# Making the sums of the down-projection's weights during the cross-attention instead of during its output projection

## The chip, the cores and the metric

The kernel runs on one core of one Trainium2 chip. A core has a matrix engine (TensorE, PE in the profile; PEld is its loading of stationary blocks), a vector engine (VectorE, DVE), an activation engine (ScalarE, ACT), GpSimd (POOL) and SyncE (SP), on whose queue all DMA transfers of this kernel are issued, in order. Each engine works through its own instructions in order and waits on semaphores. The metric is the device time of one launch in microseconds (us); the median of three runs of the kernel before is 2608.81 us (2608.45 to 2614.19).

## What is computed

Two layers on 1024 tokens of width 1024 in float32. Layer 0 mixes the tokens by attention, layer 1 by a pooling mixer; each layer then attends to 256 memory tokens and applies a gated MLP:

```python
def memory_cross_attention(h, mem_n, w_q, w_kv, w_o):
    q = (h @ w_q).reshape(b, s, X_HEADS, X_HEAD_DIM) * (X_HEAD_DIM ** -0.5)
    kv = mem_n @ w_kv
    ...
    p = jax.nn.softmax(scores, axis=-1).astype(v.dtype)
    o = jnp.einsum('bhsm,bmhd->bshd', p, v).reshape(b, s, D_MODEL)
    return o @ w_o

def conv_gated_ffn(h, w_up, conv_w, conv_b, w_down):
    u = h @ w_up
    up = jnp.pad(u, ((0, 0), (1, 1), (0, 0)))
    u = up[:, :-2] * conv_w[0] + up[:, 1:-1] * conv_w[1] + up[:, 2:] * conv_w[2] + conv_b
    gate, val = u[..., :D_FF], u[..., D_FF:]
    return (jax.nn.silu(gate) * val) @ w_down
```

`w_down` is 2816 x 1024. Each sub-layer is preceded by an RMS norm and followed by a residual add.

## The kernel before

**Products.** Every float32 product is made of three passes (`mm3`, L598): both factors are split into a high part (a copy by ACT, L513/L521) and a remainder (a subtraction by DVE, L516/L522/L525), and high x high, high x low and low x high are summed in PSUM. The up- and the down-projection of the MLP use, for 2 x 2 blocks, a scheme with seven products instead of eight. For the down-projection that scheme needs, of each of ten pairs q of 128-row blocks of `w_down` (NQ = 10), the four sums T1 to T4 of its 512-column halves: T1 = B12-B11, T2 = B22-T1, T3 = B22-B12, T4 = B21-T2. They are made once in each layer, ahead of their use, and parked in DRAM (`WT`, ten tensors of four 128x512 blocks).

**Staging.** All weights come through `scr`, a pool of six buffers of 128x1024 float32 (L506): one transfer of 512 KB on SP's queue, a high part by ACT, a remainder by DVE into one of the 20 slots R. A buffer is taken by the next `scr()` in turn, and the transfer into it waits until its last user is done. The residual rows X (eight tiles of 128x1024) stay in SBUF.

**Cross-attention** (`cross`, L990). The query projection goes over four column pieces c of `w_q` with two halves of the tokens and two blocks m each: a gemm (`cross_q`, L976) is 24 matmuls of 512 columns. After piece 0 the memory tokens are normed and turned (`memory_T`). Then eight pieces of `w_kv` (`memory_part`), the first four for the keys; each has two groups of 24 matmuls of 256 columns. Then scores, softmax, the other four pieces, and the values. In what order the instructions of this stage stand in the queues of their engines is decided at build time by a scheduler, from the order in which they are written and its own estimate of their times.

**Output projection of the cross-attention** (`ffn`, `ffn_main`, `begin`, L375). The order is written out by hand: sixteen steps, each a half row tile (n, t), n being the column half. A step's gemm is 24 matmuls into one PSUM bank; DVE adds it to X (L1102). When the second half of row tile t is done (n = 1), the finished row is written to DRAM (`rows`, L241: X to Xd, 512 KB), because the same tile is then normed in place (`norm`, L246) for the MLP; the norm thus waits for that write. ACT and POOL meanwhile make the row's mean square and its root (L582, L574, L576). In seven of the steps PE turns a normed tile by eight transposes (`turn`, L251), and DVE and ACT take the turned banks (`take1`, `take2`, L269, L274, L284). The body of a step:

```python
            gemm(n, t)
            free(n, t)
            u = turns.get(i)
            if u is not None:
                self.turn(u)
            extras.get(i, lambda: None)()
            add(n, t)
            if n:
                self.rows(t)
            ahead(i)
```

`ahead(i)` (L1234) is where the sums of `w_down` are made: at step i it takes two `scr` buffers and starts the two 512 KB loads of pair i (L1239); at step i it also makes the four sums of pair i-1 in place (L1244, DVE) and starts their four writes of 256 KB to `WT` (L1245). So steps 0 to 10 carry it. After `ahead` come `take1`, the norm and `take2` of the step on DVE's queue.

**The MLP** follows in an order that a planner (`Plan`) lays out from fixed costs. Its down-projection reads the sums back from `WT` (L1256), much later.

Of the kernel before, what the change touches and what calls it, by code (L numbers as in the profile page):

```python
# [10 lines left out]
F32 = mybir.dt.float32  # L11
F32R = mybir.dt.float32r
AF = mybir.ActivationFunctionType
OP = mybir.AluOpType
AX = mybir.AxisListType

P = 128
# [25 lines left out]
NQ = NF // 2 - 1  # L43
# [183 lines left out]
class Seven:  # L227
# [144 lines left out]
        return u.rearrange("p (t h c) -> p h t c", h=2, c=P)[:, h]  # L372


    def begin(self, gemm, add, free, between, ahead):  # L375


        late, split = self.late, self.split
        steps = ((0, 0), (0, 2), (1, 0), (1, 2), (0, 4), (1, 4), (0, 6), (1, 6),
                 (0, 1), (1, 1), (0, 3), (1, 3), (0, 5), (0, 7), (1, 5), (1, 7))  # L380
        turns = {3: 0, 4: 2, 6: 4, 8: 6, 10: 1, 12: 3, 15: 5}
        extras = {1: between, 11: lambda: self.first_load(0, 3), 12: lambda: self.first_load(1, 1),
                  13: lambda: [self.sum(0, n) for n in ("S1", "S2", "S3")],
                  14: lambda: (split(0, "A12", "A11"), late("T2", 1), late("T2", 3)),
                  15: lambda: late("T3", 1)}
        for i, (n, t) in enumerate(steps):
# [6 lines that stand above are left out]
            add(n, t)  # L393
            if n:
                self.rows(t)
            ahead(i)
            if u is not None:
                self.take1(u)
            if n:
                self.norm(t)  # L400
            if u is not None:
                self.take2(u)
# [76 lines left out]
class Kernel:  # L479
    def __init__(self, ctx, tc, a, out):  # L480
        self.ctx, self.tc, self.nc, self.a, self.out = ctx, tc, tc.nc, a, out
        pool = lambda name, **k: ctx.enter_context(tc.tile_pool(name=name, bufs=1, **k))
        self.cst = pool("cst")
        self.rp = pool("rslots")
        self.fp = pool("fp")
        self.st = pool("st")
        self.R = Slots([self.rp.tile([P, 2048], F32R, name=f"R{i}") for i in range(N_SLOTS)])
        nc = self.nc
        self.ident = self.cst.tile([P, P], F32, name="ident")
        make_identity(nc, self.ident)  # L490
        self.mh = self.cst.tile([P, 8], F32, name="mh")
        nc.vector.memset(self.mh, -0.5)

# [495 lines left out]

    def cross(self, i, hT, qT, ws):  # L990
        nc, R = self.nc, self.R
        for c in range(XH):
            if c == 1:
                mT = self.memory_T(i)
            if c:
                ws = self.cross_piece(i, c)
            for half in range(2):
                if (c, half) not in qT:
                    self.cross_q(qT, c, half, ws, hT)
                if c == XH - 1:  # L1000
                    R.put(*hT[half])
            R.put(*ws)
        kT, v, memory_part = self.memory(i, mT)
        for c in range(4):
            memory_part(c)
        kh, kl = (R.v(s, 8) for s in kT)
        vh, vl = (R.v(s, 2) for s in v)
        prs, PT, O = {}, {}, []

        def scores(t):  # L1010
            half = t // 4
            tc_ = slice((t % 4) * P, (t % 4 + 1) * P)
            s = self.psA().rearrange("p (h m) -> p h m", h=XH)
            for h in range(XH):
                qv = R.tiles[qT[h, half]].rearrange("p (m i n) -> p m i n", m=2, i=2)
                for k in range(2):
                    self.mm3(s[:, h], qv[:, k, 0, tc_], qv[:, k, 1, tc_], kh[:, 2 * h + k], kl[:, 2 * h + k],
                             k == 0, k == 1)
            nm = self.stat(4, "nm4")
            nc.vector.tensor_reduce(nm, s, axis=AX.X, op=OP.max, negate=True)  # L1020
            pr = prs[t] = self.scr()
            p3 = pr.rearrange("p (h m) -> p h m", h=XH)
            rs = self.stat(4, "sum4")
            for h in range(XH):
                nc.scalar.activation(p3[:, h], s[:, h], AF.Exp, bias=nm[:, h:h + 1], accum_out=rs[:, h:h + 1])
            ri = self.stat(4, "inv4")
            nc.vector.reciprocal(ri, rs)
            for h in range(XH):
                nc.gpsimd.tensor_scalar(p3[:, h], p3[:, h], ri[:, h:h + 1], 1.0, op0=OP.mult, op1=OP.mult)
            if t % 4 == 3:  # L1030
                R.put(*(qT[h, half] for h in range(XH)))

        def turn(t):
            if t < 2:
                PT[t] = [R.get() for _ in range(4)]
            self.transposed(prs.pop(t), self.put_T(PT[t % 2], t // 2))

        def values(half, ms):
            pt = PT[half]
            if not ms[0]:  # L1040
                O.append([R.get() for _ in range(4)])
            o = O[half]
            for m in ms:
                p = self.psB()
                cols = slice(m * P, (m + 1) * P)
                for k in range(2):
                    bh, bl = self.blk(pt, (m // 2) * 2 + k, slice(0, 512))
                    self.mm3(p, vh[:, k, cols], vl[:, k, cols], bh, bl, k == 0, k == 1)
                h, l = self.blk(o, m, slice(0, 512))
                self.hi_lo(h, l, p)  # L1050
            if ms[-1] == NK - 1:
                R.put(*pt)

        for t in range(4):
            scores(2 * t)
            memory_part(4 + t)
        for t in range(4):
            scores(2 * t + 1)
            turn(2 * t)
        values(0, (0, 1))  # L1060
        turn(1)
        values(0, (2, 3))
        turn(3)
        turn(5)
        values(0, (4, 5))
        turn(7)
        values(0, (6, 7))
        values(1, range(NK))
        R.put(*kT, *v)
        return O  # L1070


    def conv_table(self, i):
        nc, a = self.nc, self.a
        cw = self.scr()
        c3 = cw[:2 * NF, :512].rearrange("p (j c) -> p j c", j=4)
        nc.sync.dma_start(out=c3[:, :3], in_=a["ffn_conv_w"][i].rearrange("j (f c) -> f j c", c=P))
        nc.sync.dma_start(out=c3[:, 3], in_=a["ffn_conv_b"][i].rearrange("(f c) -> f c", c=P))

        def turn():  # L1080
            cp = self.psB()[:, :4 * 2 * NF].rearrange("p (j f) -> p j f", j=4)
            for j in range(4):
                nc.tensor.transpose(cp[:, j, :], c3[:, j, :], self.ident[:2 * NF, :2 * NF])
            self.cv = self.cst.tile([P, 4, 2 * NF], F32, name="conv")
            nc.vector.tensor_copy(self.cv, cp)
        return turn
# [27 lines left out]
    def ffn_main(self, i, U, X, Xd, late, begin):  # L1114
        nc, R = self.nc, self.R
        wd = self.a["ffn_w_down"][i]
        G = self.tc.dram_tile([2 * P, S], F32, name=f"G{i}")
        G7 = self.tc.dram_tile([NQ, P, 7 * 512], F32, name=f"Gs{i}")
        WT = [self.tc.dram_tile([4, P, 512], F32, name=f"Wt{i}_{q}") for q in range(NQ)]
        C, fixed, half = {}, {}, U.half  # L1120


# [107 lines left out]


        WD, raws = {}, {}

        def ahead(i):  # L1234

            if i < NQ:
                raws[i] = [self.scr() for _ in range(2)]
                for j in range(2):
                    nc.sync.dma_start(out=raws[i][j], in_=wd[(2 * i + j) * P:(2 * i + j + 1) * P, :])  # L1239
            if 0 < i <= NQ:  # L1240
                (b11, b12), (b21, b22) = ((r[:, :512], r[:, 512:]) for r in raws.pop(i - 1))
                for n, (out, p, q) in {"T1": (b11, b12, b11), "T3": (b12, b22, b12), "T2": (b22, b22, b11),
                                       "T4": (b21, b21, b22)}.items():
                    nc.vector.tensor_tensor(out=out, in0=p, in1=q, op=OP.subtract)  # L1244
                    nc.sync.dma_start(out=WT[i - 1][int(n[1]) - 1], in_=out)  # L1245

        WAT = (("B21", "B22"), ("B11",), ("T1", "T2"), ("T3", "T4"))

        def plan_W(plan, q, late):
            def fetch(j):  # L1250
# [4 lines left out]
                else:  # L1255
                    nc.sync.dma_start(out=raws[q, j].rearrange("p (n c) -> p n c", n=2),  # L1256
                                      in_=WT[q][2 * (j - 2):2 * (j - 1)].rearrange("n p c -> p n c"))

# [80 lines left out]
            plan.add("add", 1024, low, [o, *parts], parts, uses=[o], late=late)  # L1339

        def main():
            begin(ahead)
            U.H["T4"] = [R.get(), R.get()]
            plan = Plan({"DVE": 6.5, "ACT": 4.9}, {"scr": 2, "A": 2, "B": 4, "half": len(R.freed)})
            for f, js in ((0, (0, 1, 2)), (1, (0,))):
# [19 lines left out]
            for item in order:  # L1365
# [7 lines left out]
                n, f = item  # L1373
# [17 lines left out]
        with self.tc.manual_schedule():  # L1391
            main()
# [211 lines left out]
```

## Time and profile before

| | |
|---|---|
| median of three runs | 2608.81 us (2608.45 to 2614.19) |
| the profiled execution | 2610.45 us, of which the span of its instructions is 2608.7 us |
| mean granted clock of PE | 0.989 |
| output projection of the cross-attention, layer 0 | about 847 to 956 us of the span |
| the same, layer 1 | about 1853 to 1960 us |
| query projection and keys of the cross-attention, layer 0 | about 659 to 769 us |
| the same, layer 1 | about 1669 to 1774 us |

Times inside the execution are us from the start of the span. In a row of the timeline the columns are the start, the length, the engine, the line of the kernel, the operation with its output and inputs, the count, and in brackets how long the engine had been idle and what ended that. A row of the chain of waits has start, length and what it was. "SPq" is the issue of a transfer by SP, which is short; the transfer itself is "DMA" in the chain. In the table by stretches each engine has its busy time in the stretch, with the number of its instructions.

### The profile page before, as it was taken

Reading aid. Unit: us, or ns where it says so; the run is one execution under the profiler, and the core shown is the slowest. Engines: PE = TensorE matmul, PEld = TensorE weight load, DVE = VectorE, ACT = ScalarE, POOL = GpSimd, SP = SyncE. Lnnn points to the kernel's source line nnn. Section 1 sums busy time; section 2 is a strip of 40 time slices with the busy share of each in tenths; the row PEclk is TensorE's granted clock in tenths of the full one; section 3 lists DMA queues with packets and bytes.
Section 4 is the critical chain, followed back from the end, with each engine's and each line's share of the span. In section 5 each row is a group of like instructions: output and inputs, shape, how many; then the busy total and the mean of one; then the engine's idle time right before and its main releaser. Section 6 shows DMA issues by size and latency. Waiting matters only on the chain.

```text
span 2608.7 us, 36701 instructions
## 1 busy us (share of the span) xinstructions
PE 2536.9 (97%) x13577; PEld 2166.9 (83%) x13577; DVE 1911.3 (73%) x2791; ACT 1298.5 (50%) x2192; POOL 378.1 (14%) x521
## 2 busy tenths in 40 slices
PE   7999999999999999999999998999999999999998
PEld 7988888888898778888887887889778888887886
DVE  5778999974336679888888765534769988888775
ACT  4448888852236246554555424524426555555441
POOL 3664555530002000000000001102010000000001
PEclk9999999999999999999999999999999999999999
DMA  4200000031313733433348642311673343337751
GB/s 155 82 9 1 1 2 1 2 138 40 98 56 117 279 124 113 122 101 99 104 158 268 208 153 76 120 62 44 226 243 100 92 120 101 106 100 264 236 189 65
DMA packets 279945, 298.41 MB, mean 114 GB/s; under 512 B 11605, under 2 KB 225981, under 8 KB 279765
## 3 DMA queue, kind: packets, MB, share of 16 engines
q1 hardware_dynamic: 279765, 296.06, 35.3%
q8 instruction: 107, 1.75, 0.3%
q14 instruction: 73, 0.60, 0.1%
HBM read 218.85 MB, written 72.35 MB: 112 GB/s over the span
## 4 chain that ended last, share of the span: by engine, by line
PE 76%; DVE 11%; DMA 4%; ACT 4%; issue 3%; POOL 2%; SPq 0%; DVEq 0%; ACTq 0%; POOLq 0%
PE pB L603 20%; PE pB L602 20%; PE pB L601 20%; PE pB L595 3%; PE pA L603 3%; PE pA L601 3%; PE pA L602 3%; DVE nm L681 2%; PE pA L677 2%; DMA scr<-in_ffn_w_down 1%; DMA Xd<-X 1%; PE pB L908 1%; DVE PT L522 1%; POOL qn L753 1%; PE pB L909 1%
## 5 line engine op out<-in xcount | busy, mean ns | idle before, releaser
L601 PE MATMUL pB<-R,R 128*128 128x512 f32 (+1 forms) x2728 | 1023.1, 376 | 4.5 <-ACT R L521 1.9
L603 PE MATMUL pB<-R,R 128*128 128x512 f32 (+1 forms) x2748 | 1025.0, 373 | 1.7 <-DVE R L516 1.7
L602 PE MATMUL pB<-R,R 128*128 128x512 f32 (+1 forms) x2728 | 1018.0, 373 | 1.7 <-DVE R L522 1.4
L601 PEld LDWEIGHTS pB<-R,R 128*128 128x128 f32 x2728 | 515.9, 189 | 98.6 <-ACT R L521 3.1
L603 PEld LDWEIGHTS pB<-R,R 128*128 128x128 f32 x2748 | 519.5, 189 | 93.7 <-DVE R L516 2.5
L602 PEld LDWEIGHTS pB<-R,R 128*128 128x128 f32 x2728 | 516.2, 189 | 92.6 <-DVE R L522 4.0
L513 ACT ACTIVATE R<-scr 128x512 fp32r<-128x512 f32 (+2 forms) x250 | 176.0, 737 | 211.2 <-PE pB L602 68.8
L574 POOL TENSOR_SCALAR ms<-ss 128x1 f32<-128x1 f32 (+2 forms) x102 | 26.7, 262 | 1671.9 <-ACT scr L582 758.8
L516 DVE TENSOR_TENSOR R<-X,R 128x512 fp32r<-128x512 f32 x310 | 209.7, 685 | 65.7 <-ACT R L513 65.6
L513 ACT ACTIVATE R<-X 128x512 fp32r<-128x512 f32 x310 | 193.3, 630 | 82.9 <-PE pB L602 62.2
L516 DVE TENSOR_TENSOR R<-scr,R 128x512 fp32r<-128x512 f32 (+2 forms) x250 | 197.9, 821 | 19.4 <-ACT R L513 19.4
L595 PE MATMUL pB<-ident,scr 128*128 128x128 f32 x1376 | 182.3, 276 | 9.6 <-DVE scr L587 8.0
L595 PEld LDWEIGHTS pB<-ident,scr 128*128 128x128 f32 x1376 | 157.0, 142 | 36.6 <-POOL scr L687 14.8
L687 POOL TENSOR_SCALAR scr<-scr,inv 128x1024 f32<-128x1024 f32 x128 | 144.2, 1127 | 167.1 <-DVE inv L686 162.2
L522 DVE TENSOR_TENSOR PT<-pB,PT 128x512 fp32r<-128x512 f32 x256 | 163.8, 680 | 3.4 <-ACT PT L521 2.4
L365 ACT COPY scr<-pB 128x512 f32<-128x512 f32 x132 | 77.4, 586 | 177.5 <-PE pB L603 175.2
L684 ACT ACTIVATE scr<-pA,nm 128x1024 f32<-128x1024 f32 x128 | 142.9, 1117 | 44.6 <-DVE nm L681 42.5
L1296 DVE TENSOR_TENSOR X<-pB,X 128x512 f32<-128x512 f32 x144 | 99.2, 690 | 87.8 <-PE pB L603 85.3
L601 PE MATMUL pA<-R,R 128*128 128x512 f32 (+1 forms) x448 | 156.3, 349 | 6.0 <-ACT R L521 2.1
L521 ACT ACTIVATE R<-pB 128x512 fp32r<-128x512 f32 (+1 forms) x182 | 94.5, 551 | 129.9 <-PE pB L603 82.1
L681 DVE TENSOR_REDUCE nm<-pA 128x1 f32<-128x1024 f32 x128 | 156.1, 1219 | 0.9 <-PE pA L677 0.5
L603 PE MATMUL pA<-R,R 128*128 128x512 f32 (+1 forms) x448 | 155.3, 347 | 1.1 <-DVE R L522 0.8
(138 smaller groups left out, 3647.9 us busy)
## 6 DMA issues: line engine op xcount, KB each, us to landing
X<-in_ffn_w_up SPq DMA_DIRECT2D x82, 512.0 KB
scr<-in_ffn_w_down SPq DMA_DIRECT2D x64, 512.0 KB
Gs<-X SPq DMA_DIRECT2D x100, 256.0 KB
scr<-Gs SPq DMA_DIRECT2D x56, 384.0 KB
Wt<-scr SPq DMA_DIRECT2D x80, 256.0 KB
scr<-Wt SPq DMA_DIRECT2D x40, 512.0 KB
scr<-in_xattn_w_kv SPq DMA_DIRECT2D x32, 512.0 KB
scr<-Gs SPq DMA_DIRECT2D x28, 512.0 KB
```

The source lines that it names most:

```text
L513: self.nc.scalar.activation(hi, src, AF.Copy)
L516: self.nc.vector.tensor_tensor(out=lo, in0=src, in1=hi.bitcast(F32), op=OP.subtract)
L521: nc.scalar.activation(hi, src, AF.Copy)
L522: nc.vector.tensor_tensor(out=lo, in0=src, in1=hi.bitcast(F32), op=OP.subtract)
L595: self.nc.tensor.transpose(p[:, k, :], src[:, b * P:(b + 1) * P], self.ident)
L601: mm(out, ah, bh, start=start, stop=False)
L602: mm(out, ah, bl, start=False, stop=False)
L603: mm(out, al, bh, start=False, stop=stop)
L681: nc.vector.tensor_reduce(nm, s, axis=AX.X, op=OP.max, negate=True)
L684: nc.scalar.activation(pr, s, AF.Exp, bias=nm, accum_out=rs)
L687: nc.gpsimd.tensor_scalar(pr, pr, ri, 1.0, op0=OP.mult, op1=OP.mult)
L1296: nc.vector.tensor_tensor(out=x, in0=banks[b], in1=x, op=OP.add)
```

## The change

The function `ahead` leaves `ffn_main` and becomes `down_sums`, which `cross` calls at its start. It returns a function that does on each call what a step did before: the loads of the next pair, and the sums and writes of the pair before. It is called after each `cross_q` that `cross` issues (seven: the first half of piece 0 is issued ahead of `cross`) and after each of the first four `memory_part` (four), eleven calls in each layer. The sums themselves and their number are as before; `ffn_main` gets the list through `self.WT`.

```diff
-    def begin(self, gemm, add, free, between, ahead):
+    def begin(self, gemm, add, free, between):
...
             add(n, t)
             if n:
                 self.rows(t)
-            ahead(i)
             if u is not None:
                 self.take1(u)
...
+        self.WT = {}
...
     def cross(self, i, hT, qT, ws):
         nc, R = self.nc, self.R
+        ahead = self.down_sums(i)
         for c in range(XH):
             if c == 1:
                 mT = self.memory_T(i)
...
                 if (c, half) not in qT:
                     self.cross_q(qT, c, half, ws, hT)
+                    ahead()
...
         for c in range(4):
             memory_part(c)
+            ahead()
...
+    def down_sums(self, i):
+        nc, wd = self.nc, self.a["ffn_w_down"][i]
+        WT = self.WT[i] = [self.tc.dram_tile([4, P, 512], F32, name=f"Wt{i}_{q}") for q in range(NQ)]
+        raws, todo = {}, iter(range(NQ + 1))
+
+        def ahead():
+            q = next(todo, None)
+            if q is None:
+                return
+            if q < NQ:
+                raws[q] = [self.scr() for _ in range(2)]
+                for j in range(2):
+                    nc.sync.dma_start(out=raws[q][j], in_=wd[(2 * q + j) * P:(2 * q + j + 1) * P, :])
+            if q:
+                (b11, b12), (b21, b22) = ((r[:, :512], r[:, 512:]) for r in raws.pop(q - 1))
+                for n, out, x, y in ((0, b11, b12, b11), (2, b12, b22, b12), (1, b22, b22, b11), (3, b21, b21, b22)):
+                    nc.vector.tensor_tensor(out=out, in0=x, in1=y, op=OP.subtract)
+                    nc.sync.dma_start(out=WT[q - 1][n], in_=out)
+        return ahead
...
-        WT = [self.tc.dram_tile([4, P, 512], F32, name=f"Wt{i}_{q}") for q in range(NQ)]
+        WT = self.WT.pop(i)
...
-            begin(ahead)
+            begin()
```

More of the change, by code (lines that the diff above doesn't have):

```diff
@@ L1232, in ffn_main @@
         WD, raws = {}, {}
[L1234 to L1245, printed above, removed]
         WAT = (("B21", "B22"), ("B11",), ("T1", "T2"), ("T3", "T4"))
```

## The prediction

> **What bounds the kernel now.** The page first:
>
> ```profile
> span 2608.7 us, 36701 instructions
> PE 2536.9 (97%) x13577; PEld 2166.9 (83%) x13577; DVE 1911.3 (73%) x2791; ACT 1298.5 (50%) x2192; POOL 378.1 (14%) x521
> PE 76%; DVE 11%; DMA 4%; ACT 4%; issue 3%; POOL 2%; SPq 0%; DVEq 0%; ACTq 0%; POOLq 0%
> ```
>
> PE is busy for 97% of the span and holds 76% of the chain of waits. The change leaves PE's instructions and their order alone (the built programs show the same list), so it can only act where PE waits or runs slowly. The table by stretches says where that is: first the output projections of both layers, then the query projection and the key pieces, layer 0 and layer 1.
>
> ```profile
> core 0: us, PE busy (x) PEld busy (x) DVE busy (x) ACT busy (x) POOL busy (x), PEclk, DMA share, GB/s
> 853.50:956.40 102.90, 94.55 (x419) 77.05 (x417) 63.73 (x90) 22.74 (x41) 9.29 (x16) 0.93 0.68 235
> 1858.90:1959.80 100.90, 93.35 (x418) 76.11 (x418) 63.66 (x90) 22.83 (x41) 8.74 (x16) 0.95 0.70 241
> 659.00:745.00 86.00, 85.50 (x388) 70.28 (x386) 24.65 (x31) 23.34 (x34) 0.74 (x2) 1.00 0.20 64
> 745.00:769.00 24.00, 23.99 (x200) 23.98 (x200) 10.68 (x15) 6.92 (x13) 0.00 (x0) 1.00 0.42 132
> 1669.00:1750.00 81.00, 80.50 (x366) 66.16 (x364) 24.06 (x31) 23.19 (x35) 0.74 (x2) 1.00 0.21 70
> 1750.00:1774.00 24.00, 24.00 (x200) 24.00 (x201) 10.58 (x15) 7.37 (x13) 0.00 (x0) 1.00 0.42 131
> ```
>
> In the output projections PE idles 8.35 and 7.55 us, its granted clock is 0.93 and 0.95, and the DMA engines are busy 0.68 and 0.70 of the time. In the cross-attention PE hardly idles (0.5 us), its clock is 1.00, DMA stands at 0.20 and 0.42, and DVE at 24.65 of 86 us. So work leaves a crowded stage for an empty one.
>
> What PE waits for is shown by its waits in the two output projections (total, times, longest) and by one piece of the chain:
>
> ```profile
> PE pB L251 <- DVE X L246: 8.4, 3, 3.8
> PE pB L251 <- DVE X L246: 7.5, 4, 3.1
> ...
> 869.79 0.70 DVE X L1102
> 870.51 6.36 DMA Xd<-X
> 877.00 1.30 DVE X L246
> ...
> 878.34 1.26 PE L251 MATMUL pB<-ident,X 128*128 128x128 f32 x8 [2.23 <-DVE X L246]
> 880.34 0.63 PE L603 MATMUL pB<-R,R 128*128 128x512 f32 x1
> 880.77 0.63 PE L601 MATMUL pB<-R,R 128*128 128x512 f32 x1
> 884.21 0.39 PE L602 MATMUL pB<-R,R 128*128 128x512 f32 x1
> 884.44 0.40 PE L603 MATMUL pB<-R,R 128*128 128x512 f32 x1
> ```
>
> A row is finished (L1102), its write to Xd takes 6.36 us, only then may it be normed in place, and PE's transposes wait 2.23 us for that. After such a wait matmuls start every 0.43 us instead of every 0.23 us for some 4 us: each wait is paid about twice.
>
> **The loss in numbers.** L1102 marks the end of each gemm, as long as DVE is free for it:
>
> ```profile
> 852.87 0.69 DVE L1102 TENSOR_TENSOR X<-pB,X 128x512 f32<-128x512 f32 x1 [2.63 <-PE pB L603]
> 858.94 0.68 DVE L1102 TENSOR_TENSOR X<-pB,X 128x512 f32<-128x512 f32 x1
> 864.35 0.69 DVE L1102 TENSOR_TENSOR X<-pB,X 128x512 f32<-128x512 f32 x1 [1.95 <-PE pB L603]
> 869.79 0.69 DVE L1102 TENSOR_TENSOR X<-pB,X 128x512 f32<-128x512 f32 x1 [0.36 <-PE pB L603]
> 892.38 0.69 DVE L1102 TENSOR_TENSOR X<-pB,X 128x512 f32<-128x512 f32 x1 [0.37 <-PE pB L603]
> 898.70 0.69 DVE L1102 TENSOR_TENSOR X<-pB,X 128x512 f32<-128x512 f32 x1 [0.66 <-PE pB L603]
> 955.75 0.69 DVE L1102 TENSOR_TENSOR X<-pB,X 128x512 f32<-128x512 f32 x1
> 1858.26 0.69 DVE L1102 TENSOR_TENSOR X<-pB,X 128x512 f32<-128x512 f32 x1 [2.24 <-PE pB L603]
> 1959.10 0.69 DVE L1102 TENSOR_TENSOR X<-pB,X 128x512 f32<-128x512 f32 x1
> ```
>
> A step without a turn takes 869.79-864.35 = 5.44 us; one with a turn 898.70-892.38 = 6.32, so a turn is 0.88; the first gap, with the turn of the convolution's table in it, is 6.07, or 0.63 more. From the first add to the last lie 15 gemms, six turns and that table: 15x5.44 + 6x0.88 + 0.63 = 87.5 us. The trace has 955.75-852.87 = 102.9 and 1959.10-1858.26 = 100.8. Lost: 15.4 + 13.3 = 28.7 us. (Cross-check for layer 0: 8.35 idle and 0.07x102.9 = 7.2 of clock make 15.6.)
>
> **What is removed.** In both layers together:
>
> ```profile
> L1244 DVE TENSOR_TENSOR scr<-scr x80: 678/692/721, 859.5 to 1927.9; 128x512 f32<-128x512 f32 x80
> L1239 SPq DMA_DIRECT2D scr<-in_ffn_w_down x40: 327/424/1325, 842.1 to 1920.2; - x40
> L1245 SPq DMA_DIRECT2D Wt<-scr x80: 319/422/1329, 860.2 to 1928.6; - x80
> ...
> 916.27 6.42 DMA scr<-in_ffn_w_down
> 950.31 0.69 DVE L1102 TENSOR_TENSOR X<-pB,X 128x512 f32<-128x512 f32 x1 [2.35 <-PE pB L603]
> 953.77 1.28 DVE L246 SCALAR_TENSOR_TENSOR X<-X,rs,scr 128x1024 f32<-128x1024 f32 x1 [2.77 <-DMA Xd<-X]
> ```
>
> Per layer: 40 subtractions (40x0.69 = 27.7 us of DVE), 20 loads and 40 writes, 21 MB. Two effects go with them. The write of a row no longer shares the DMA engines with 2 MB in each step: late in the stage, with that traffic over, the norm starts 953.77-950.31-0.69 = 2.77 us after the add instead of 7. And DVE no longer stands before a load: at 916.27 the chain runs through a load of 6.42 us, behind which the takes of the turned banks and the next add were queued.
>
> Does a wait stay? From the end of a gemm: add 0.69, write 2.77, norm 1.28, with some 0.1 of gaps 4.85 us. Between that gemm and the turn that needs the row, PE has at least one other gemm, 5.44 us. So no wait should be left, with 0.6 us to spare. What is late next is the row's root on ACT and POOL: in the quiet row the write, not the root, came last, so the root takes less than 2.77. The three subtractions of an odd turn (3x0.69) and its two remainders fit into the 5.44 us as well. The spare is thin, and two loads of the up-projection now start near the write of row 1, so I leave 0.5 us a layer: 28.7 - 1.0 = 27.7 us gained, between 28.7 (no wait, no slow clock) and 8.4 + 7.5 = 15.9 (the idle alone goes).
>
> **What is added.** The same 120 transfers and 80 subtractions, in the cross-attention. DVE has room: 24.65 + 10.68 + 27.7 = 63 of 110 us. DMA too: 21 MB more over 110 us is 190 GB/s on top of 64 and 132. The danger is order. In the built program DVE's subtractions stand between the drains of the query gemms; each waits for its load, and the drain behind it waits along.
>
> ```profile
> 707.01 0.69 DVE L525 SCALAR_TENSOR_TENSOR R<-pB,R 128x512 fp32r<-128x512 f32 x1 [3.38 <-ACT R L524]
> 712.46 0.69 DVE L525 SCALAR_TENSOR_TENSOR R<-pB,R 128x512 fp32r<-128x512 f32 x1 [4.75 <-ACT R L524]
> 742.61 3.49 DVE L522 TENSOR_TENSOR R<-scr,R 128x1024 fp32r<-128x1024 f32 x3 [2.26 <-ACT R L521]
> 756.66 0.42 DVE L522 TENSOR_TENSOR R<-pB,R 128x256 fp32r<-128x256 f32 x1 [2.46 <-ACT R L521]
> 759.54 0.42 DVE L522 TENSOR_TENSOR R<-pB,R 128x256 fp32r<-128x256 f32 x1 [2.46 <-ACT R L521]
> ```
>
> A drain comes every 5.44 us with 4.75 us of idle before it; four subtractions fit in 2.8. There are four banks, so a drain may be three gemms (16 us) late before PE stops. SP's queue and `scr`: the eleven calls take 20 of the buffers that the weights use, and a weight load now stands behind the writes of a pair. The tightest such load is the fourth key piece: its buffer comes free with the three remainders at 742.61+3.49 = 746.1; with 6.42 us of landing and 2.3 for high and low part it is there at 755. Groups of that stage are 759.54-756.66 = 2.88 us apart, and the fourth piece begins at about 762. Even at the worst landing nothing is late by these rows, so the cost is 0 at best; for what I can't see (queueing of loads behind writes) I take 0.5 us a layer, and 7.3 us a layer as its upper end: the landing excess of 6.42-2.77 = 3.65, twice.
>
> On that queueing the Trainium skill speaks against the change: in "DMA: Bandwidth & Descriptors", section "Queues, rings and completion order", it says that each DMA engine consumes a queue's descriptors in ring order. A weight load issued behind four writes would then land after them as well. The trace agrees: 6.36 us behind 2 MB, 2.77 us alone; the sum stays, since the worst landing is in it.
>
> **Sum.** 2610.45 (the profiled execution, 1.74 more than its span, and 1.64 over the median) - 28.7 + 1.0 + 1.0 = 2583.8; against the median, 2608.8 - 26.7 = 2582.1 us. I predict 2582.
>
> **Rivals.** (1) Slower: the `scr` loop paces PE. A call needs load, sums and writes before its buffers serve again: 2.77 + 2.8 + 6.36 = 11.9 us if calls don't overlap, and eleven have the 110 us of query projection and keys, 10 each. Then 22x(11.9-10) = 42 is lost against 27 won: 2624. It decides from 11.6 us a call, where 22x1.6 = 35 eats the gain and 8 more. For it: one SP queue, six buffers. Against: the built order issues a second pair's loads ahead of the first pair's last writes, so two calls overlap. 7%. (2) The key pieces become DMA-bound: 1 MB of weights, 1 MB loaded and 1 MB written in 5.76 us is more than the 241 GB/s moved at a share of 0.70, or 344 at full share: 3.15 MB take 9.1 us, 3.4 too many, in four pieces and two layers 27 us: 2609, no change. Against: the pieces' loads start earlier, where PE needs 22 us for each query piece. 5%. (3) The slow clock is not the waits' doing and stays: only 8.4 + 7.5 of idle go, 2593. For it: 2.23 us is a short wait to slow a clock. Against: it is 1.00 in every stretch above without waits. 6%.
>
> The skill's page "TensorE: Matmul & The Clock Gate", section "Part 1: The HAM clock gate (the "warmup" mystery)", says that the clock halves after an idle window of about 3.4 us. By that rule a 2.23 us wait need not slow it, which is the third rival; the trace, slow right behind that wait, disagrees.
>
> (4) The write stays slow without the traffic, and only the waits for loads in DVE's queue go (the longest waits, 3.8 and 3.1, each paid twice: 13.8): 2595. Against: the 2.77. 4%.
>
> **How the numbers follow.** Forecast 78% (2578 to 2590). The range 2577 to 2600 takes in rivals 3 and 4 and the upper end of the added cost (2582 + 2x6.8 = 2596); below it ends 5 us under the forecast, since no more than 28.7 is there to be had and runs differ by a few us. A measurement of this kernel can tell about 0.3%, 8 us, from no change. Faster than 2601: 78+6+4 = 88%; within: rival 2, 5%; slower: 7%.
>
> **What would show it.** In the output projections: adds 5.44 and 6.32 us apart throughout, 88 to 89 us from first to last, clock 1.00, DMA share about 0.2, the norm 2.8 to 3.1 us after its add. In the cross-attention: the subtractions of `down_sums` between the drains, DMA share 0.6 or more, PE's idle still under 1 us and adds and drains 5.44 apart. Waits of PE for remainders of weights there, or for drains, would prove me wrong; so would norms that still start 5 us after their add.

## The result, and the profile after

| | before | after |
|---|---|---|
| median of the runs, us | 2609.29 (2608.45 to 2614.19, 4 runs) | 2585.19 (2584.72 to 2586.67, 4 runs) |
| after to before | | 0.9905, 95% interval 0.9888 to 0.9922 |
| span of the profiled execution, us | 2608.7 | 2583.3 |
| first to last add of the output projection, layer 0 / layer 1, us | 102.9 / 100.8 | 88.2 / 88.15 |

The changed kernel is 0.95% faster, 24.1 us by the medians and 25.4 by the spans. Line numbers shift with the moved code: the add of the output projection is L1126 now (L1102 before), the subtractions L1093 (L1244), their writes L1094 (L1245), the loads L1089 (L1239), the drain of a query gemm L524 (L525), the add of the down-projection L1306 (L1296).

The first lines of its page, span and busy time (share of the span, number of instructions):

```profile
span 2583.3 us, 36696 instructions
...
PE 2524.0 (98%) x13577; PEld 2156.9 (83%) x13577; DVE 1910.4 (74%) x2791; ACT 1298.5 (50%) x2192; POOL 379.5 (15%) x521
```

DVE and ACT are busy for as long as before: nothing was saved, only moved. PE shows 13 us less busy time for the same 13577 matmuls. Of these, 11.7 us are in the two output projections (94.55 and 93.35 before, 88.08 and 88.09 in the next table), whose granted clock was 0.93 and 0.95: the same work ran more slowly there.

The table by stretches of the changed kernel, for the same four stages as in the prediction (both output projections, the query projection and the key pieces of layer 0):

```profile
core 0: us, PE busy (x) PEld busy (x) DVE busy (x) ACT busy (x) POOL busy (x), PEclk, DMA share, GB/s
852.30:940.60 88.30, 88.08 (x419) 72.79 (x418) 37.26 (x50) 22.44 (x41) 7.79 (x16) 1.00 0.18 60
1845.00:1933.20 88.20, 88.09 (x419) 72.75 (x418) 37.33 (x50) 22.44 (x41) 7.78 (x16) 1.00 0.18 60
658.00:744.00 86.00, 85.49 (x388) 70.29 (x387) 48.02 (x66) 24.58 (x36) 2.45 (x4) 1.00 0.81 283
744.00:768.00 24.00, 24.00 (x201) 24.00 (x202) 12.89 (x19) 6.62 (x13) 0.00 (x0) 1.00 0.66 217
```

In the output projections PE idles 0.2 and 0.1 us where it idled 8.35 and 7.55, its clock is 1.00, and the DMA share fell from 0.7 to 0.18. In the cross-attention DMA's share rose from 0.20 to 0.81 and from 0.42 to 0.66, and DVE's busy time doubled in the first stretch, while PE's column stands to the hundredth: 85.49 of 86.00 (85.50 before), 24.00 of 24.00.

Adds and norms of the changed kernel's first output projection, by their start; in brackets the idle time of DVE before the instruction and what ended it:

```profile
851.67 0.69 DVE L1126 TENSOR_TENSOR X<-pB,X 128x512 f32<-128x512 f32 x1 [2.63 <-PE pB L602]
...
866.66 1.29 DVE L246 SCALAR_TENSOR_TENSOR X<-X,rs,scr 128x1024 f32<-128x1024 f32 x1 [2.81 <-DMA Xd<-X]
...
904.86 0.69 DVE L1126 TENSOR_TENSOR X<-pB,X 128x512 f32<-128x512 f32 x1 [3.01 <-PE pB L602]
909.14 1.28 DVE L246 SCALAR_TENSOR_TENSOR X<-X,rs,scr 128x1024 f32<-128x1024 f32 x1 [3.59 <-DMA Xd<-X]
910.34 0.68 DVE L1126 TENSOR_TENSOR X<-pB,X 128x512 f32<-128x512 f32 x1
917.11 0.69 DVE L1126 TENSOR_TENSOR X<-pB,X 128x512 f32<-128x512 f32 x1 [1.30 <-PE pB L602]
...
939.89 0.69 DVE L1126 TENSOR_TENSOR X<-pB,X 128x512 f32<-128x512 f32 x1
```

The norm now starts 2.8 to 3.6 us after its add (909.14 is 3.59 behind the end of the add at 904.86), where the second row of the kernel before took 6.5 (877.00 against 869.79+0.69). The last add is at 939.89, 88.2 us behind the first. The step 917.11-910.34 = 6.77 is the one that is still too long beside the 6.34 or so of the other steps with a turn (one add that DVE makes late, 7.03 us and then 4.87, aside), a residue of some 0.4 us behind the latest norm, 3.59. Right behind that row's write, SP issues two loads of the up-projection (905.99 and 906.47).

And DVE in the query projection of the changed kernel, where the subtractions went:

```profile
722.14 0.69 DVE L524 SCALAR_TENSOR_TENSOR R<-pB,R 128x512 fp32r<-128x512 f32 x1 [4.15 <-ACT R L523]
...
727.58 0.69 DVE L1093 TENSOR_TENSOR scr<-scr 128x512 f32<-128x512 f32 x1 [4.75 <-DMA scr<-in_ffn_w_down]
728.19 0.68 DVE L524 SCALAR_TENSOR_TENSOR R<-pB,R 128x512 fp32r<-128x512 f32 x1
```

DVE stands before loads here too, 4.75 us at 727.58 with the drain of 728.19 queued behind. That drain is 0.6 us later than 5.44 behind its predecessor, and PE does not notice: the query gemms change between banks of PSUM. Here the wait of DVE costs nothing; how far that cover reaches is tested below.

### The profile page after: what moved, and what is told of

It is laid out like the page before. It is cut to its first block, busy times and chain, and to the rows that moved or that the text cites. A ratio compares the mean times of both kernels' runs of the same rounds, so it can differ in the third digit from the quotient of the medians.

```text
span 2583.3 us, 36696 instructions
## 1 busy us (share of the span) xinstructions
PE 2524.0 (98%) x13577; PEld 2156.9 (83%) x13577; DVE 1910.4 (74%) x2791; ACT 1298.5 (50%) x2192; POOL 379.5 (15%) x521
## 5 line engine op out<-in xcount | busy, mean ns | idle before, releaser
L594 PE MATMUL pB<-ident,scr 128*128 128x128 f32 x1376 | 183.0, 277 | 9.8 <-DVE scr L586 8.0
L594 PEld LDWEIGHTS pB<-ident,scr 128*128 128x128 f32 x1376 | 157.1, 142 | 37.5 <-POOL scr L686 15.2
L1306 DVE TENSOR_TENSOR X<-pB,X 128x512 f32<-128x512 f32 x144 | 99.2, 690 | 87.6 <-PE pB L602 85.1
```

Of the source, the lines that this page charges most:

```text
L594: self.nc.tensor.transpose(p[:, k, :], src[:, b * P:(b + 1) * P], self.ident)
L1306: nc.vector.tensor_tensor(out=x, in0=banks[b], in1=x, op=OP.add)
```

## The experiments

Three questions were open: which part of the moved work did the harm in the output projection (the sums that hold DVE, the amount of transfers, SP's queue standing, the order within one DMA queue); whether the amount acts by a threshold or in proportion; and how deep the cover in the cross-attention is. Each kernel's runs are compared with runs of the kernel before that were timed with them on the same chip; medians of different sets are not compared closely, since the kernel before alone has 2609.29 to 2613.45 in four sets. "First to last" is that of the adds, layer 0 / layer 1.

| kernel | in the output projection | first to last, us | median, us | to before (95%) |
|---|---|---|---|---|
| before | loads, sums, their writes | 102.9 / 100.8 | 2613.45, 2612.94, 2611.39 | |
| e1_no_sums | loads, writes | 99.5 / 97.3 | 2605.97 | 0.9977 (0.9964 to 0.9990) |
| e9_both_again | loads, writes without a wait | 99.5 / 96.0 | 2606.09 | 0.9971 (0.9961 to 0.9982) |
| e10_row_on_act | as before, row by another queue | 103.1 / 100.3 | 2616.19 | 1.0012 (1.0001 to 1.0022) |
| e11_three_quarters | loads, half the writes | 89.8 / 89.1 | 2588.34 | 0.9914 (0.9893 to 0.9935) |
| e3_loads_again | loads | 87.85 / 87.9 | 2584.68 | 0.9896 (0.9876 to 0.9916) |
| e4_writes_again | writes | 87.8 / 88.1 | 2588.61 | 0.9918 (0.9895 to 0.9940) |
| e2_sums_again | sums | 88.4 / 88.4 | 2586.27 | 0.9904 (0.9881 to 0.9928) |
| e7_no_lag | nothing | 88.1 / 88.2 | 2587.97 | 0.9903 (0.9887 to 0.9920) |
| e8_in_key_pieces | nothing | 88.1 / 88.2 | 2593.98 | 0.9929 (0.9914 to 0.9944) |

(The three medians of before belong to the three sets in which e1 to e4, then e9, e10, e7 and e8, and last e11 were timed.)

**The sums taken out of the old place.**

```
--- before, ahead()
+++ e1_no_sums
-                    nc.vector.tensor_tensor(out=out, in0=p, in1=q, op=OP.subtract)
                     nc.sync.dma_start(out=WT[i - 1][int(n[1]) - 1], in_=out)
```

> The kernel before with the 80 subtractions left out: the halves of the raw weights are parked where the sums belong, loads and writes stay in the output projections as they were. First-to-last add of the output projections was 102.9 and 100.8 us, 87.5 without a wait. Theory (two effects, the row's write slowed by the traffic and DVE standing before loads): the standing goes, the slow write stays, so about half of the 28.7 us comes back: 94 to 97 us in each layer, norms still 5 us or more after their add, about 2595. Rival A (only DVE's standing counts): 88 to 89 us, 2584. Rival B (only the traffic counts): 100 us or more, 2605 to 2609.

Both layers came out between the theory and rival B, 99.5 and 97.3 us. So the sums and DVE's standing were worth 3.4 + 3.5 = 6.9 us of the 28.7, and the transfers alone keep 12.0 + 9.8 = 21.8. The theory had given the two effects about half each. (This kernel leaves the sums out, so what it computes is not the result; it is there for its time.)

**Each kind of work alone in the new kernel.** A hook at the old place in `begin` does one of three things:

```
--- after, begin() with ahead(i) behind rows(t) again
+++ e2_sums_again: four subtractions of halves of X[7], into scratch, at steps 1 to 10
+            nc.vector.tensor_tensor(out=out, in0=x, in1=y, op=OP.subtract)
+++ e3_loads_again: two loads at steps 0 to 9
+            nc.sync.dma_start(out=self.scr(), in_=wd[(2 * i + j) * P:(2 * i + j + 1) * P, :])
+++ e4_writes_again: four writes at steps 1 to 10
+            nc.sync.dma_start(out=spare[i - 1][n], in_=X[7][:, n % 2 * 512:(n % 2 + 1) * 512])
```

> The changed kernel with 40 more subtractions a layer in steps 1 to 10 of the output projection, from a residual row that is at rest, into scratch, without any transfer (nothing reads them). Theory (DVE's 27.7 us a layer were not the cost, its waits for loads and the traffic were): first-to-last add stays at 88 to 90 us, 2585 to 2589. Rival (DVE's time itself was short in the stage): 92 us or more, waits of PE for norms come back, 2593 or more.

> The changed kernel with only the loads put back beside the output projection: two of 512 KB at each of steps 0 to 9, into scratch that nothing reads; no subtraction, no write. Theory (the traffic slows the row's write): half the traffic, so the write of a row lands between 2.77 and 6.36 us, about 4.5; that is over the spare of 0.6 us by 1.1, at about six turns and paid twice: 93 to 101 us first to last, 2595 to 2605. Rival (only the waits of DVE for a load did the harm): 88 to 90 us, 2585 to 2589.

> The changed kernel with only writes put back beside the output projection: four of 256 KB at each of steps 1 to 10, from a residual row at rest to a spare area that nothing reads; no load, no subtraction. Theory (traffic slows the row's write whichever way it goes): as with the loads alone, 93 to 101 us first to last, 2595 to 2605. Rival A (it is the writes alone, since they stand before the row's write in one queue): as slow as the kernel before or nearly, 2600 or more, while the loads alone cost under 4 us. Rival B (it is the loads alone): under 90 us here, 2585 to 2589.

The table by stretches of the first output projection, of e2_sums_again, e3_loads_again and e4_writes_again in turn:

```profile
853.90:942.30 88.40, 88.10 (x418) 72.72 (x418) 60.84 (x90) 22.45 (x41) 11.13 (x16) 1.00 0.18 60
```

```profile
852.30:940.20 87.90, 87.90 (x418) 72.65 (x418) 37.23 (x50) 22.44 (x41) 7.76 (x16) 1.00 0.45 156
```

```profile
855.80:943.60 87.80, 87.80 (x418) 72.79 (x418) 37.31 (x50) 22.44 (x41) 7.77 (x16) 1.00 0.47 168
```

None costs anything in the stage: 24 us more of DVE work (60.84 against 37.26) adds 0.2 us, and half the transfers of either kind, which raise the DMA share from 0.18 to 0.45 or 0.47, add none at all. PE's clock stays at 1.00. So the theory failed for e3 and e4: half the traffic does not slow the row's write by half.

The total of e4 is 3.4 us over the changed kernel's in spite of that. Its first add already comes at 855.14, 3.5 us later than 851.67, so the difference arose ahead of the stage. There the edit did something that was not meant: the scheduler moved four of the 40 writes of each layer up (36 are issued in the output projection), in layer 0 to 602.6, 651.6, 660.3 and 722.8, the last three inside the query projection or just ahead of it. The drain of a query gemm (L525) then comes 7.93 us behind its predecessor instead of 5.44 (665.81 against 657.88), and PE stands for it:

```profile
666.55 0.79 PE L601 MATMUL pB<-R,R 128*128 128x512 f32 x1 [1.98 <-DVE R L525]
```

Layer 1 has such a wait of 1.5 us. The changed kernel, whose subtractions stand in the same place, has none.

**All the traffic, without a wait in it.** Loads and writes of e3 and e4 together. No write depends on a load, so SP no longer stands at one for long: in layer 0 its waits that end with a landing are 1.0 us at most.

> The changed kernel with both loads (two of 512 KB at steps 0 to 9) and writes (four of 256 KB at steps 1 to 10, from a residual row at rest to a spare area) put back beside the output projection; nothing reads them, no write waits for a load, no subtraction. Alone, either half cost nothing there (87.8 to 88.1 us first to last). Theory (a backlog: 2.1 MB a step and half a row's 0.5 MB need 2.36 MB in about 5.8 us, 405 GB/s, at or above what the DMA engines moved at their best, so the row's write finds the queue full): norms 5 us or more after their add, 96 us or more first to last, 2600 or more. Rival (not the amount, but SP's queue standing at writes that wait for their load): 88 to 89 us, 2585 to 2589.

The table by stretches of e9_both_again, both output projections, and pieces of its chain of waits (start, duration, what):

```profile
853.90:953.40 99.50, 91.82 (x418) 75.04 (x418) 37.03 (x50) 22.64 (x41) 7.79 (x16) 0.97 0.66 233
1861.00:1957.00 96.00, 90.58 (x418) 73.59 (x418) 36.95 (x50) 22.54 (x41) 7.78 (x16) 0.98 0.72 256
```

```profile
870.16 0.70 DVE X L1127
...
870.88 6.83 DMA Xd<-X
...
877.84 1.30 DVE X L246
```

DVE is no busier than in the changed kernel (37.03 us), and yet the stage takes 99.5 and 96.0 us. The write of the second row takes 6.83 us from its issue, right behind the add, to its landing. The amount by itself costs 12.0 + 8.5 = 20.5 of the 28.7 us again. That agrees with e1, where the writes still waited for the loads (21.8); SP's queue standing at such a wait counts for little.

**The row's write by a queue of its own.** In the kernel before, ACT issues it.

```
--- before, Seven.rows()
+++ e10_row_on_act
-        self.nc.sync.dma_start(out=self.Xd[t * P:(t + 1) * P, :], in_=self.X[t])
+        self.nc.scalar.dma_start(out=self.Xd[t * P:(t + 1) * P, :], in_=self.X[t])
```

> The kernel before, with the write of a finished row issued from ScalarE instead of SyncE, so that it goes by another DMA queue; loads, sums and their writes stay in the output projections on SyncE's queue. Theory A (the write stands behind earlier transfers of its own queue): it lands in about 3 to 4 us, the norms start 3 to 4 us after their add, most of the slow-write part is gone: 90 to 94 us first to last, 2588 to 2595. Theory B (the DMA engines are shared by all queues and are full): it lands as late as before, 5 us or more, 99 to 103 us first to last, 2603 to 2610.

It is theory B by the time. The chain of waits of e10_row_on_act at the first two rows:

```profile
866.06 4.41 DMA Xd<-X
...
871.80 0.70 DVE X L1102
...
872.52 6.77 DMA Xd<-X
...
879.42 1.30 DVE X L246
```

The second row's write takes 6.77 us on its own queue, 6.36 on the shared one: another queue does not bring it forward. That fits theory B, engines that are full for all queues. It does not show that the place in a queue has no effect, for the edit changes a second thing: SP no longer stands at the row's write until the add is done, and issues the next loads earlier. The first row shows it. On the shared queue the loads are issued behind its write (865.44 behind 865.07), and its norm starts 3.11 us after the add; here they are issued ahead of it (863.79, the write 866.06), and it takes 4.41 us. How much of the 6.36 us is order within the shared queue stays open.

**Three quarters of the traffic.** Both loads and two of the four writes.

> The changed kernel with three quarters of the traffic put back beside the output projection: both loads (1 MB) and two of the four writes (0.5 MB) at each step, nothing reads them. Half of it, loads or writes, cost nothing (87.8 to 88.1 us first to last), all of it 8 to 11 us a layer. Theory (a backlog with a threshold: 1.57 MB and half a row's 0.52 make 1.84 MB in about 5.8 us, 315 GB/s, under the 400 or so that the engines moved at their best, so the queue is empty again when the next row is written): norms 2.8 to 3.8 us after their add, 88 to 90 us first to last, 2583 to 2590. Rival (the write slows in proportion to what else is moved, and the loss begins where its spare of 0.6 us is gone): norms 4.5 us or more after their add, 91 to 96 us, 2592 to 2602.

The first four norms of e11_three_quarters in the first output projection (the later ones wait 2.8 to 3.2 us):

```profile
868.66 1.28 DVE L246 SCALAR_TENSOR_TENSOR X<-X,rs,scr 128x1024 f32<-128x1024 f32 x1 [3.09 <-DMA Xd<-X]
876.53 1.28 DVE L246 SCALAR_TENSOR_TENSOR X<-X,rs,scr 128x1024 f32<-128x1024 f32 x1 [5.51 <-DMA Xd<-X]
888.69 1.28 DVE L246 SCALAR_TENSOR_TENSOR X<-X,rs,scr 128x1024 f32<-128x1024 f32 x1 [3.12 <-DMA Xd<-X]
900.67 1.28 DVE L246 SCALAR_TENSOR_TENSOR X<-X,rs,scr 128x1024 f32<-128x1024 f32 x1 [3.31 <-DMA Xd<-X]
```

A threshold, not a proportion. All norms that wait but one start 2.8 to 3.3 us after their add, as with no traffic to speak of. (In the second output projection the same row is late, 4.64 us, and the others take 2.8 to 3.5.) The one that is late (5.51) belongs to the second row, the only place, while the traffic runs, where two rows end in steps that follow each other (steps 2 and 3): there 1.57 + 0.52 = 2.1 MB must move in 5.44 us, 385 GB/s. Between other rows lie two steps, 2x1.57 + 0.52 = 3.7 MB in 5.44 + 6.34 = 11.8 us, 311 GB/s. Its lateness makes up most of the 1.6 to 2.3 us that this kernel's stage takes beyond 87.5. With the whole traffic it is 2.1 + 0.52 = 2.6 MB in 5.44 us, 480 GB/s, and 2x2.1 + 0.52 = 4.7 MB in 11.8, 400 GB/s. What the engines moved is in the transfer view of e9_both_again, its window from 850 to 955 us in equal slices:

```profile
GB/s 347 201 0 0 0 0 253 209 380 417 408 417 400 305 53 264 265 402 419 407 408 405 415 399 175 181 233 304 404 366 293 364 65 0 0 0 0 147 53 112
```

No slice (2.6 us each) goes above 419 GB/s. So 311 GB/s between two rows' writes leave the write prompt, while 385 and more make it late: the limit lies between these two, somewhat below the best slice. The order of prompt and late norms in e9_both_again agrees. They start 3.13, 6.99, 3.16, 5.86, 3.08 and 5.79 us after their adds, since a late row stretches the steps behind it: from the second row's add to the third's it is 887.60-870.16 = 17.4 us instead of 11.8, and 4.7 MB in that time are 270 GB/s; from the third to the fourth it is 11.8 again, 400 GB/s.

**The cover in the cross-attention.** In e7_no_lag the sums of a pair are made in the call that loads it; in e8_in_key_pieces the calls are taken from the query projection and put behind the key pieces, three for each.

```
--- after, down_sums() and cross()
+++ e7_no_lag
-            if q:
-                (b11, b12), (b21, b22) = ((r[:, :512], r[:, 512:]) for r in raws.pop(q - 1))
+            if True:
+                (b11, b12), (b21, b22) = ((r[:, :512], r[:, 512:]) for r in raws.pop(q))
...
-                    nc.sync.dma_start(out=WT[q - 1][n], in_=out)
+                    nc.sync.dma_start(out=WT[q][n], in_=out)
+++ e8_in_key_pieces
                     self.cross_q(qT, c, half, ws, hT)
-                    ahead()
...
             memory_part(c)
-            ahead()
+            for _ in range(3):
+                ahead()
```

> The changed kernel with the sums of a pair made in the call that loads it, not one call later, so DVE stands before each load in the cross-attention. Theory (the cover is deep: a drain may be 16 us late before PE stops; a load of up to 6.4 us and 2.8 us of sums make it 4.5 us late at most): nothing is lost, 2583 to 2589, the stretch from the start of the query projection to the first add of the output projection within 1 us of the changed kernel's. Rival (the lag of one call is what keeps the scratch loop from pacing PE): 2 us or more a call, 22 calls, 2625 or more.

> The changed kernel with all calls behind the four key pieces, three behind each, none in the query projection. Theory (the price of the cover if it is gone: 21 MB of pairs and sums and 4 MB of weights at some 390 GB/s take 64 us where the key pieces take 23; part runs on into the scores): 20 to 40 us lost a layer, 2625 to 2665. Rival (the cross-attention takes it anywhere, the place inside it does not matter): under 2595.

The total of e7_no_lag shows no loss: 0.9903 of the kernel before, where the changed kernel has 0.9905. From the first drain of the query projection to the first add of the output projection layer 0 takes 854.50-658.83 = 195.7 us against 851.67-658.14 = 193.5, and layer 1 takes 207.0 against 205.8. So in the profiled execution there is a price of 2.1 and 1.3 us, more than the 1 allowed for, and far from the 2 us a call of the rival. PE's waits of e7_no_lag in layer 0 (total, times, longest) name it:

```profile
PE pB L594 <- DVE R L524: 1.4, 1, 1.4
...
PE pB L600 <- DVE R L524: 0.9, 1, 0.9
```

Two drains of query gemms came too late for PE, by 1.4 and 0.9 us; the changed kernel has no wait for L524. So DVE standing before a load can use up the cover. That it is the lag of one call that prevents this is not shown, for e4_writes_again has the lag and waits 1.98 us for the same drain. In both kernels the drain is only 1.1 to 2.5 us late when PE stops (665.42-658.83 = 6.59 in e7_no_lag), not 16. At these places the memory tokens are turned between the query gemms (L594, L595 in e4), and the turned tiles stand in banks of the same pool (pB): the four banks are not all there for the gemms.

e8_in_key_pieces loses 8.8 us by the medians, 6.3 when each kernel is set against the kernel before of its own set (0.9929 and 0.9905), where 40 to 80 were expected. One reason is that the program's order is not the order of the text: the subtractions of layer 0 start at 680.9, in the middle of the query projection, since the scheduler moves them up to where DVE is free. The run therefore tests a later and denser place, not the key pieces alone. Its table by stretches for the key pieces and what follows, layer 0 and layer 1:

```profile
745.00:770.00 25.00, 24.36 (x202) 24.15 (x202) 19.33 (x29) 6.37 (x12) 0.00 (x0) 1.00 0.97 341
770.00:800.00 30.00, 27.86 (x230) 27.45 (x229) 14.70 (x22) 14.05 (x37) 6.46 (x12) 1.00 0.52 171
1735.00:1760.00 25.00, 24.56 (x200) 24.03 (x199) 19.55 (x29) 7.08 (x12) 0.00 (x0) 1.00 0.90 314
1760.00:1790.00 30.00, 26.23 (x190) 25.36 (x188) 13.34 (x18) 12.62 (x34) 6.66 (x8) 0.89 0.48 160
```

In layer 0 the DMA engines are full in the key pieces (0.97, 341 GB/s) and PE idles 0.64 us there; it idles 2.14 in the stretch behind, where the changed kernel has 1.06 of 30. From first drain to first add the layer loses 195.6-193.5 = 2.1 us. Layer 1 loses three times as much, 212.2-205.8 = 6.4: behind the key pieces PE waits 3.77 us at once for the exponentials of the scores (L1027), 1.7 in the changed kernel, and the clock of the stretch falls to 0.89. So nearly full DMA engines beside the keys went with a loss of 2.1 and 6.4 us a layer. That the transfers alone made it is not shown, because here the scheduler also put some of PE's matmuls into another order.

## Why the prediction was right, step by step

**The loss and its end: right.** 28.7 us were put down as lost in the output projections, 1.0 of it to remain. The adds now span 88.2 and 88.15 us, so 14.7 + 12.7 = 27.4 came back and 0.7 + 0.65 remain, against 0.5 a layer. The signs announced are there, clock 1.00 and DMA share 0.18; the norms start 2.8 to 3.6 us behind their add, where 2.8 to 3.1 had been announced.

**Which of the two effects: right in kind, wrong in size.** The prediction named the slow write of the row and DVE's standing before loads, and in its fourth rival priced the standing at 13.8 us by the two longest waits, each paid twice. It is 6.9 (e1_no_sums), or 28.7-20.5 = 8.2 (e9_both_again). The two longest waits were priced whole to the loads. At the same rows PE still waits without any sum (e1_no_sums): 1.38 of the 3.81 us in layer 0, 1.96 of the 3.13 in layer 1. That didn't touch the sum, which took both effects away together.

**The order in the queue: read from too little.** The prediction read 6.36 us behind 2 MB and 2.77 alone as a write that stands behind earlier transfers of its queue. The two numbers are right, but they don't tell order in a queue from full engines: by its own queue the write takes 6.77 us (e10_row_on_act). The Trainium skill, "DMA: Bandwidth & Descriptors", section "Queues, rings and completion order", says that each DMA engine takes a queue's descriptors in ring order; no run here contradicts that, and the first row of e10_row_on_act, late once loads were issued ahead of it, is in keeping with it. But the prediction's "the trace agrees" was too much for its two numbers.

**The rivals.** The slow clock went with the waits, so the third fell. The fourth fell with the writes: 2.8 to 3.6 us. The first, the scratch loop, had eleven calls at 10 us each in mind; even without the lag they cost 2.1 and 1.3 us a layer. The second, DMA-bound key pieces, gave 3.4 us to each piece, 13.6 a layer. With the engines nearly full in the key pieces (0.97 and 0.90 in e8_in_key_pieces) 2.1 and 6.4 us a layer were lost.

**What is added: right in size, with a thinner cover than was argued.** 0.5 us a layer had been kept for queueing; layer 0 takes 851.67-658.14 = 193.53 us from first drain to first add, and took 852.87-659.36 = 193.51; layer 1 takes 205.8 and took 205.2. But the argument, that a drain may be 16 us late before PE stops, is wrong: PE waited for a drain that was 2.5 us late in e4_writes_again and for one that was 1.1 us late in e7_no_lag. That the changed kernel has no such wait is in part luck of the order that the scheduler found; four writes more in that stage made one.

**The sum: 3 us too low,** 2582 against 2585.2. The stages that the change touches are right within a microsecond. The largest difference lies elsewhere: from the last add of the output projection to the first of the down-projection some 425 us later.

```profile
1365.55 0.68 DVE L1306 TENSOR_TENSOR X<-pA,X 128x512 f32<-128x512 f32 x1
1932.52 0.69 DVE L1126 TENSOR_TENSOR X<-pB,X 128x512 f32<-128x512 f32 x1
2358.11 0.69 DVE L1306 TENSOR_TENSOR X<-pA,X 128x512 f32<-128x512 f32 x1
```

```profile
1379.58 0.68 DVE L1296 TENSOR_TENSOR X<-pA,X 128x512 f32<-128x512 f32 x1
...
2383.16 0.68 DVE L1296 TENSOR_TENSOR X<-pA,X 128x512 f32<-128x512 f32 x1
```

After (the first fence) that is 1365.55-939.89 = 425.7 and 2358.11-1932.52 = 425.6 us, before (the second, from 955.75 and 1959.10) 423.8 and 424.1: together 3.4 us against the changed kernel. The same stretch in the other profiles, layer 0 and layer 1: e1 425.4 and 423.7, e2 424.75 and 425.2, e3 424.05 and 425.4, e4 424.0 and 425.4, e7 425.5 and 425.55, e8 423.9 and 425.8, e9 425.9 and 425.1, e10 426.1 and 425.9, e11 424.9 and 424.2. Kernels with the sums at the old place and at the new show both ends of it, and two layers of one run differ by 1.9. PE waits 1.7 and 2.1 us in that stretch before, 3.3 and 3.3 after. So it looks like scatter, and the profile of before happened to have the low end twice. (Of the spans' 25.4 us, 27.4 - 0.6 - 3.4 = 23.4 are thus told; the other 2.0 lie outside these stretches, 1.2 of them ahead of the first query drain.) Whether the new place adds something on the average wasn't settled: it would take many profiles of each.

## What to carry to other kernels

Work on an idle engine is not free if its transfers are ahead of something else's: before parking loads and writes in a stage, add up what must move between two transfers that the stage waits for, and compare it with what the engines moved at their best. Leave some room: here 311 GB/s between two such transfers cost nothing, 385 made the transfer late, and the best slice was 419. Then look at the built program and not at the text, for a scheduler may have moved the work to another stage. And a stage that shows no wait is not yet a stage with room: the cross-attention took 21 MB a layer with hardly a loss, but ended 3.5 us later in a kernel whose scheduler had moved four more writes ahead (e4_writes_again).

## What the runs showed of the hardware

**A wait's length alone does not tell whether the clock slows.** PE in e9_both_again at its second and at its sixth row, and in e11_three_quarters ahead of the down-projection; the first column is the start:

```profile
879.18 1.50 PE L251 MATMUL pB<-ident,X 128*128 128x128 f32 x8 [2.68 <-DVE X L246]
...
880.97 0.63 PE L602 MATMUL pB<-R,R 128*128 128x512 f32 x1
881.40 0.63 PE L603 MATMUL pB<-R,R 128*128 128x512 f32 x1
...
935.27 1.06 PE L251 MATMUL pB<-ident,X 128*128 128x128 f32 x8 [2.52 <-DVE X L246]
...
936.40 0.39 PE L602 MATMUL pB<-R,R 128*128 128x512 f32 x1
936.62 0.39 PE L603 MATMUL pB<-R,R 128*128 128x512 f32 x1
```

```profile
1366.29 0.50 PE L601 MATMUL pA<-R,R 128*128 128x512 f32 x1 [1.12 <-ACT R L513]
...
1368.31 0.63 PE L602 MATMUL pB<-R,R 128*128 128x512 f32 x1
1368.74 0.63 PE L603 MATMUL pB<-R,R 128*128 128x512 f32 x1
```

After a wait of 2.68 us matmuls start every 0.43 us, after one of 2.52 every 0.22 to 0.23, and after one of 1.12 every 0.43 again. So no length of a wait divides the slow cases from the others in these traces. The kernel before showed the slow ones after 2.23 us, for some 4 us. A wait can thus be paid about twice, as the prediction had it, or once, as the late norm of e11_three_quarters was (1.25 us of waiting, matmuls every 0.23 to 0.24 us behind it). The Trainium skill, in "TensorE: Matmul & The Clock Gate", section "Part 1: The HAM clock gate (the "warmup" mystery)", gives an idle window of about 3.4 us for the slowing; the waits here are shorter, and some of them slowed the clock. What besides the length decides is not shown here.

**Loss against traffic.** In the first output projection the DMA share was 0.18, 0.45, 0.61 and 0.66 with none, the loads, three quarters and all of the moved transfers, and the time beyond 87.5 us was 0.7, 0.4, 2.3 and 12.0. The share looks alike in the last two: it is a mean over the stage, and the late transfers stretch the stage that it is taken over.
